# Seven block products for eight in the two feed-forwards of a decoder layer

## The chip, the cores and the metric

The kernel is one program on one core of a Trainium2 chip. A time is what the device takes for one execution, in microseconds (us). TensorE (PE) multiplies matrices into PSUM, which has eight banks of 512 columns; VectorE (DVE) and ScalarE (ACT) do the elementwise work, GpSimd (POOL) a few small operations; SyncE (SP) issues the loads and stores. "PEld" in the profile is TensorE's loading of the stationary operand.

## The reference

One decoder layer for 512 tokens of width 1024: a feed-forward, a mixing layer (attention and a gated delta rule), cross-attention into 256 memory tokens, and a second feed-forward, each between two RMS norms. Everything is float32. The part that matters:

```
def swiglu(x, w_gate, w_up, w_down):
    return (jax.nn.silu(x @ w_gate) * (x @ w_up)) @ w_down        # D_FF = 2816

f = swiglu(rms_norm(h, ffn1_pre_norm[l]), ffn1_w_gate[l], ffn1_w_up[l], ffn1_w_down[l])
h = h + FFN_RESIDUAL_WEIGHT * rms_norm(f, ffn1_post_norm[l])
...
f = swiglu(rms_norm(h, ffn2_pre_norm[l]), ffn2_w_gate[l], ffn2_w_up[l], ffn2_w_down[l])
h = h + FFN_RESIDUAL_WEIGHT * rms_norm(f, ffn2_post_norm[l])
```

## The kernel before

A float32 product is made of three float32r products. `split` (L393) writes `hi` = the operand rounded (ACT) and `lo` = operand - `hi` (DVE); `proj_t` (L486) and `nat_mm` (L504) then multiply hi by hi, hi by lo and lo by hi. So every weight block of 128 x 1024 is loaded by `wload` (L429, three `raw` buffers) and split by `wsplit` (L437) into a pair `wh`, `wl`, of which there are four (`bufs=4`).

A feed-forward is `ffn` (L575). The 2816 hidden columns are 22 chunks of 128. For each chunk, gate and up are two weight blocks, each taken by `proj_t`: 8 slices of the width x 3 matmuls, with the weight slice (128 x 128) stationary and 512 tokens moving, into one bank from `acc` (L370: banks 0 to 5 in turn). In the first feed-forward `lead_in` (L635) does chunks 0 and 1 slice by slice, as x and the weights arrive, and chunk results are later scaled by the row `rb`, since x goes in without its norm. In the second one, chunks 0 and 1 run in two halves of 256 tokens (`HALVES`, L573). `finish` (L580) makes silu(gate) x up of a chunk (tanh on ACT, the rest on DVE) and splits it into `hh` and `hl`.

The down projection is `nat_product` (L509): the hidden chunk is stationary (128 tokens at a time), 512 output columns move. For each of two halves n of the output it goes through 11 weight blocks (two chunks each), for four token tiles t, with four banks accumulating; the last four blocks of n = 1 (`ntail`) are walked one token tile after another. When a bank is complete, `evac` in `residual_epilogue` (L547) squares it for the norm, multiplies it by the gain (`fg`), and with n = 1 done adds the two halves into `h`. Then `next_norm` (L678) and `prenorm` (L467) normalise the tile for the next layer, transpose it on TensorE into banks 6 and 7 (`ptr`), and split it into the four tiles `xt00` to `xt11` (`new_xT`, L458).

Other temporaries are slots of 128 x 512 from a ring of 54 (`u` takes the oldest free one, `fr` gives it back).

No order is written out by hand in the feed-forwards. Every instruction is recorded (the helper's line, L273, is what the profile shows for all of them, so rows are told apart by tile names), and `Issue.settle` (L229) lays them out with costs of its own: a list order for each engine, the instruction on the longest remaining path first, over ten rounds. On the chip each engine then runs its list in order, waiting on semaphores.

## Time and profile before

| | |
|---|---|
| median of 3 runs | 1206.58 us (1205.96 to 1206.93) |
| the profiled execution | 1206.45 us, span 1204.7 us |
| mean granted TensorE clock | 0.999 |
| busy: PE, PEld, DVE, ACT | 1187.5, 989.9, 644.7, 482.0 us |
| matmuls | 6290 |
| first feed-forward | from 6.1 to about 370 us |
| second feed-forward | from about 838 us to the end |

The profile is of one execution. A row of grouped instructions gives the line, the engine, the operation, what it writes and reads, shapes, count, total busy time, mean time of one in ns, and idle time before. Instructions on one engine overlap a little: a busy time runs from an instruction's start to its end, and the next may start earlier. The spacing of starts is read from the order of time.

### The profile page before, as it was taken

The numbers are of one execution on the slowest core, as the hardware profiler recorded it, in microseconds if no ns is written. First come the engines' busy times: TensorE is split into PE (matmuls) and PEld (weight loads), VectorE is DVE, ScalarE is ACT, GpSimd is POOL, SyncE is SP. The second block draws the span as 40 slices with busy tenths as digits, with TensorE's granted clock in tenths as the row PEclk, the third lists the DMA queues.
The fourth block names the chain that finished last, engine by engine and source line by source line (L and its number), as shares of the span: only waits on it lengthen the run. The fifth ranks groups of instructions, "written<-read, shape, count | busy, mean of one in ns | idle before, by whom it ended". The sixth has DMA issues, their size and how long they took to land.

```text
span 1204.7 us, 15978 instructions
## 1 busy us (share of the span) xinstructions
PE 1187.5 (99%) x6290; PEld 989.9 (82%) x6290; DVE 644.7 (54%) x1206; ACT 482.0 (40%) x982; POOL 46.2 (4%) x66
## 2 busy tenths in 40 slices
PE   7999999999999999999999999999999999999997
PEld 6888888888888887887778988888888888888886
DVE  5655454532237977759974955547433443432223
ACT  6323232321225573568863644444323232322211
POOL 0000000000001010101000000002000000000000
PEclk9999999999999999999999999999999999999999
DMA  8333323232433333112242462222323323232321
GB/s 292 113 95 98 105 88 105 97 114 89 121 87 103 126 93 93 56 24 85 81 149 71 139 198 84 73 85 70 106 94 98 101 92 104 97 114 88 105 70 70
DMA packets 48156, 122.61 MB, mean 102 GB/s; under 512 B 9744, under 2 KB 16272, under 8 KB 48080
## 3 DMA queue, kind: packets, MB, share of 16 engines
q1 hardware_dynamic: 47568, 121.45, 31.9%
q8 instruction: 49, 0.80, 0.3%
q0 software_dynamic: 512, 0.13, 0.1%
q14 instruction: 27, 0.22, 0.1%
HBM read 117.11 MB, written 4.33 MB: 101 GB/s over the span
## 4 chain that ended last, share of the span: by engine, by line
PE 89%; DVE 6%; ACT 3%; DMA 1%; POOL 1%; issue 1%; SPq 0%; DVEq 0%; POOLq 0%; ACTq 0%
PE psum L273 89%; DVE p L273 1%; DVE wl L273 1%; POOL smalls L273 1%; DVE h L273 1%; DVE xn L273 1%; DVE pt L273 1%; ACT pt L273 0%; DVE xt L273 0%; DMA mr<-in_mem_dram 0%; ACT wh L273 0%; ACT p L273 0%; DVE smalls L273 0%; ACT u L273 0%; DMA w<-in_f1a_dram 0%
## 5 line engine op out<-in xcount | busy, mean ns | idle before, releaser
L273 PE MATMUL psum<-xt,wh 128*128 128x512 f32 (+1 forms) x2000 | 591.4, 379 | 6.3 <-ACT wh L273 6.3
L273 PEld LDWEIGHTS psum<-xt,wh 128*128 128x128 f32 x2000 | 365.9, 189 | 72.1 <-ACT wh L273 6.6
L273 ACT ACTIVATE wh<-raw 128x1024 fp32r<-128x1024 f32 x197 | 208.9, 1061 | 524.7 <-PE psum L273 274.9
L273 DVE TENSOR_TENSOR wl<-raw,wh 128x1024 fp32r<-128x1024 f32 x197 | 240.9, 1223 | 281.9 <-ACT wh L273 280.7
L273 PE MATMUL psum<-xt,wl 128*128 128x512 f32 (+1 forms) x984 | 371.2, 382 | 0.0
L273 PEld LDWEIGHTS psum<-xt,wl 128*128 128x128 f32 x984 | 185.7, 189 | 33.6 <-DVE wl L273 0.4
L273 PE MATMUL psum<-wl,hh 128*128 128x512 f32 x352 | 137.1, 389 | 0.0
L273 PE MATMUL psum<-wh,hl 128*128 128x512 f32 x352 | 137.0, 389 | 0.0
L273 PE MATMUL psum<-wh,hh 128*128 128x512 f32 x352 | 137.0, 390 | 0.0
L273 PEld LDWEIGHTS psum<-wl,hh 128*128 128x128 f32 x352 | 66.1, 188 | 13.7
L273 PEld LDWEIGHTS psum<-wh,hl 128*128 128x128 f32 x352 | 66.1, 188 | 13.6
L273 PEld LDWEIGHTS psum<-wh,hh 128*128 128x128 f32 x352 | 66.1, 188 | 13.5
L273 POOL TENSOR_TENSOR smalls<-smalls,mhalf 128x1 f32<-128x1 f32 (+1 forms) x38 | 31.5, 829 | 700.8 <-DVE smalls L273 700.5
L273 PE MATMUL psum<-wh,xt 128*128 128x512 f32 x128 | 45.4, 412 | 0.1
L273 DVE SCALAR_TENSOR_TENSOR hv<-s,psum 128x512 f32<-128x512 f32 x22 | 15.1, 688 | 51.6 <-PE psum L273 51.4
L273 DVE TENSOR_TENSOR tu<-psum,rb 128x512 f32<-128x512 f32 x22 | 15.2, 690 | 48.9 <-PE psum L273 48.9
L273 ACT ACTIVATE u<-psum 128x512 f32<-128x512 f32 x32 | 19.0, 594 | 49.3 <-PE psum L273 49.2
L273 DVE TENSOR_TENSOR tg<-psum,rb 128x512 f32<-128x512 f32 x22 | 15.2, 690 | 41.1 <-PE psum L273 41.1
L273 ACT ACTIVATE hh<-hv 128x512 fp32r<-128x512 f32 x44 | 27.4, 623 | 14.2 <-DVE hv L273 14.2
L273 DVE TENSOR_TENSOR hl<-hv,hh 128x512 fp32r<-128x512 f32 x44 | 30.1, 685 | 0.0
L273 DVE TENSOR_TENSOR fg<-psum,gbc 128x512 f32<-128x512 f32 x32 | 21.9, 686 | 13.1 <-ACT u L273 13.1
L273 PEld LDWEIGHTS psum<-wh,xt 128*128 128x128 f32 x128 | 23.4, 189 | 4.3 <-DVE sgz L273 0.4
(234 smaller groups left out, 1356.1 us busy)
## 6 DMA issues: line engine op xcount, KB each, us to landing
raw<-in_f2gu_dram SPq DMA_DIRECT2D x44, 512.0 KB, 3.5
raw<-in_f1gu_dram SPq DMA_DIRECT2D x40, 512.0 KB, 3.6
raw<-in_f1d_dram SPq DMA_DIRECT2D x22, 512.0 KB, 3.5
raw<-in_f2d_dram SPq DMA_DIRECT2D x22, 512.0 KB, 3.5
raw<-in_wmt_dram SPq DMA_DIRECT2D x21, 512.0 KB, 3.5
raw<-in_wmn_dram SPq DMA_DIRECT2D x8, 512.0 KB, 3.5
raw<-in_wout_dram SPq DMA_DIRECT2D x8, 512.0 KB, 3.5
raw<-in_wkvk_dram SPq DMA_DIRECT2D x8, 512.0 KB, 3.5
```

The costliest lines, as they stand in the source:

```text
L273: r = call(*args, **kw)
```

## The change

Two matrices cut into 2 x 2 blocks can be multiplied with seven block products instead of eight, at the price of sums of blocks before and after (Winograd's form of Strassen's scheme: four sums on each side, seven products). The change does so in two places of both feed-forwards.

*Down projection.* `nat_product` is replaced by `down_seven` for all 22 chunks. The first 16 chunks are eight pairs: the left operand's blocks are 256 tokens x one chunk, the right one's one chunk x 512 columns. All eight banks accumulate at once: a (P1 and on), b, c, d, two token tiles each. A first pass over the eight pairs makes four of the products, a second pass, which loads three quarters of the weights again, the other three. The remaining six chunks follow as before, into the same banks, now with all four token tiles and both halves n complete only at the end. The loads of the passes go into the space of `xt00` to `xt11`, which gate and up no longer need (`homes`; pair 0 of the first pass uses the `raw` buffers). Hidden chunks of the pairs stay unsplit until then (`hfs`), and `down_sums` makes the sums of their blocks.

*Gate and up.* Chunks 4 and 5, 8 and 9, 12 and 13, 16 and 17 are made by `seven`, once for gate and once for up: blocks of 128 hidden columns x half the width, and half the width x 256 tokens. Its matmuls have 256 moving columns, 12 to a product. The sums of x are made once per feed-forward, by `seven_k` from the first one's arriving x (which now is scaled by the gain in place and kept) and by `seven_x` from copies of the normalised x that `prenorm` leaves (`keep`, a further ACT copy of each transposed bank). The sums of the weights are made on DVE in the `raw` buffers.

The core of the diff; `...` marks what is left out (helpers that pick halves and quarters of a tile, the loops that free slots, and `seven_x`, which does what `seven_k` does in additions of 512 and splits of 256):

```diff
+NPAIR = 8
+QUADS = (4, 8, 12, 16)
...
-    def prenorm(src, g, dst):
+    def prenorm(src, g, dst, keep=None):
...
+            if keep:
+                A.activation(keep(j), tp, AF.Copy)
             split(dst(j, 0), dst(j, 1), t3)
...
+    def seven_k(xk_):
+        parts = [[[u(F32R, "sx") for _ in range(2)] for _ in range(2)] for _ in range(4)]
+        for k in range(4):
+            a11, a21 = (xk_[k][:, hs] for hs in HALVES)
+            a12, a22 = (xk_[4 + k][:, hs] for hs in HALVES)
...
+            V.tensor_tensor(s1, a21, a22, ALU.add)
+            V.tensor_tensor(s2, s1, a11, ALU.subtract)
+            V.tensor_tensor(s3, a11, a21, ALU.subtract)
+            V.tensor_tensor(s4, a12, s2, ALU.subtract)
+            for i, x_ in enumerate((s1, s2, s3, s4)):
+                split(*(quarter(parts[i][q][k // 2], k % 2) for q in range(2)), x_)
...
+    def seven(wb, wa, xT, sx):
+        right, left = wload(wa), wload(wb)
+        b12, b22, b11, b21 = right[:, 0:512], right[:, 512:1024], left[:, 0:512], left[:, 512:1024]
...
+        w0, w1, w2, w3 = pair(), pair(), pair(), pair()
+        t2 = u(s="t2")
+        split(*half(w0, 0), b11)
+        V.tensor_tensor(b11, b12, b11, ALU.subtract)
+        V.tensor_tensor(t2, b22, b11, ALU.subtract)
+        split(*half(w0, 1), t2)
+        V.tensor_tensor(b12, b22, b12, ALU.subtract)
+        split(*w1, left)
+        V.tensor_tensor(t2, b21, t2, ALU.subtract)
+        split(*w2, right)
+        split(*half(w3, 0), t2)
...
+        a_, b_, c_ = acc(), acc(), acc()
...
+        product(a_, half(w0, 0), plain(0, top), True)
+        A.activation(p1, pa, AF.Copy)
+        product(b_, half(w0, 1), summed(1), True)
+        V.tensor_tensor(u2, pb, p1, ALU.add)
+        product(c_, half(w1, 0), summed(0), True)
+        A.activation(p5, pc, AF.Copy)
+        product(a_, half(w1, 1), plain(1, top), False)
+        A.activation(quarter(out_[0], 0), pa, AF.Copy)
+        product(b_, half(w2, 0), summed(2), False)
+        V.tensor_tensor(u3, pb, p1, ALU.add)
+        V.tensor_tensor(quarter(out_[1], 1), u3, p5, ALU.add)
+        product(c_, half(w2, 1), summed(3), False)
+        V.tensor_tensor(quarter(out_[1], 0), pc, u2, ALU.add)
+        product(b_, half(w3, 0), plain(1, low), False)
+        V.tensor_tensor(quarter(out_[0], 1), pb, p1, ALU.add)
...
+    def down_seven(hfs, hT, wd, evac):
+        a = [acc(), acc()]
+        b = [bank(7), acc()]
+        c = [acc(), acc()]
+        d = [bank(6), acc()]
...
+        for p in range(NPAIR):
+            left, right = ((load if p else wload)(wd[n, p]) for n in range(2))
...
+            V.tensor_tensor(b12, b12, b11, ALU.subtract)
+            V.tensor_tensor(b22, b22, b12, ALU.subtract)
+            V.tensor_tensor(b21, b21, b22, ALU.subtract)
+            w11, w4 = halves(wsplit(left))
+            w1, w2 = halves(wsplit(right))
+            x1, x2, s12, _ = hfs[p]
+            own, sums = parts(x1[:, 256:512], x2[:, 0:256]), parts(s12)
...
+            product(a, own, 0, w11, p == 0)
...
+            product(b, sums, 256, w2, p == 0)
...
+            product(c, sums, 0, w1, p == 0)
...
+            product(d, own, 256, w4, p == 0)
...
+        for p in range(NPAIR):
+            left, right = load(wd[0, p][:, 512:1024]), load(wd[1, p])
...
+            V.tensor_tensor(b12, b22, b12, ALU.subtract)
+            w21, _ = halves(wsplit(left, n=512))
+            w3, w22 = halves(wsplit(right))
+            _, x2, _, s34 = hfs[p]
+            own, sums = parts(x2[:, 256:512]), parts(s34)
+            product(a, own, 0, w21)
+            product(b, sums, 0, w3)
+            product(c, sums, 256, w22)
...
+        w = {(i, n): wblock(wd[n, NPAIR + i]) for i in (rest - 2, rest - 1) for n in (0, 1)}
+        for t in range(NT):
+            for n in (1, 0):
+                for i in (rest - 2, rest - 1):
+                    others(t, n, i, w[i, n], i == rest - 1)
...
+                if more is None:
+                    evac(n, t, ps)
+                else:
+                    V.tensor_tensor(more, ps, more, ALU.add)
+                    evac(n, t, more)
...
+            if len(hfs) < 2 * NPAIR:
+                hfs.append(hv)
+                return
...
+        while i < NFF:
+            if i in QUADS:
+                pg, pu = (seven(wgu[2 * i + j], wgu[2 * i + 2 + j], xT, sx) for j in range(2))
+                for j in range(2):
+                    finish(pg[j], pu[j], True)
+                i += 2
+                if i > max(QUADS):
...
+                    down_sums()
+                continue
...
-        nat_product(
-            list(range(NFF)),
...
+        down_seven(hfs[::2], hT, wd, residual_epilogue(gpost, 0.5, nxt, final))
...
-            fr(xr, wr)
+            fr(wr)
+            V.tensor_scalar(xr, xr, gcol[:, k : k + 1], None, ALU.mult)
```

## Rows read from the trace of the kernel before

**Rows 1.** The page, part 1: busy us (share of the span) xinstructions.

```profile
PE 1187.5 (99%) x6290; PEld 989.9 (82%) x6290; DVE 644.7 (54%) x1206; ACT 482.0 (40%) x982; POOL 46.2 (4%) x66
```

**Rows 2.** The chain that ended last: start us, length us, what.

```profile
6.11 349.65 PE psum L273 x1536
...
844.90 353.52 PE psum L273 x1621
```

**Rows 3.** Windows: stretch, its length, busy us (x) of each engine, PEclk, DMA share, GB/s.

```profile
25.00:250.00 225.00, 225.00 (x999) 186.49 (x998) 121.53 (x156) 71.22 (x89) 0.56 (x2) 1.00 0.32 102
...
850.00:1068.00 218.00, 218.00 (x1007) 182.45 (x1006) 89.30 (x105) 64.50 (x83) 0.00 (x0) 1.00 0.32 102
1078.00:1198.00 120.00, 120.00 (x531) 99.39 (x530) 33.67 (x37) 25.38 (x34) 2.02 (x3) 1.00 0.26 85
```

**Rows 4.** What PE waited for: us in total, times, longest us.

```profile
PE psum L273 <- ACT wh L273: 6.3, 2, 6.1
```

**Rows 5.** PE in order of time, 512 columns: start us, us, instruction xcount.

```profile
990.16 0.61 PE L273 MATMUL psum<-xt,wh 128*128 128x512 f32 x2
...
990.84 0.61 PE L273 MATMUL psum<-xt,wh 128*128 128x512 f32 x2
```

**Rows 6.** PE in order of time, 256 columns (six matmuls between these starts).

```profile
842.55 0.40 PE L273 MATMUL psum<-xt,wh 128*128 128x256 f32 x2
...
843.27 0.40 PE L273 MATMUL psum<-xt,wh 128*128 128x256 f32 x2
```

**Rows 7.** DVE in order of time, first feed-forward: start us, us, instruction [idle before].

```profile
31.37 1.23 DVE L273 TENSOR_TENSOR wl<-raw,wh 128x1024 fp32r<-128x1024 f32 x1 [2.49 <-ACT wh L273]
32.51 0.68 DVE L273 TENSOR_TENSOR tg<-psum,rb 128x512 f32<-128x512 f32 x1
33.12 0.68 DVE L273 TENSOR_TENSOR tu<-psum,rb 128x512 f32<-128x512 f32 x1
...
107.35 0.69 DVE L273 TENSOR_TENSOR tu<-psum,rb 128x512 f32<-128x512 f32 x1 [2.69 <-PE psum L273]
108.08 0.69 DVE L273 SCALAR_TENSOR_TENSOR hv<-s,tu 128x512 f32<-128x512 f32 x1
```

**Rows 8.** DVE groups by shape: xcount | busy us, mean ns | idle before, releaser.

```profile
L273 DVE TENSOR_TENSOR wl<-raw,wh 128x1024 fp32r<-128x1024 f32 x197 | 240.9, 1223 | 281.9 <-ACT wh L273 280.7 <-DMA raw<-in_wmt_dram 0.8
...
L273 DVE TENSOR_TENSOR v<-psum,v 128x256 fp32r<-128x256 f32 x8 | 3.3, 416 | 0.1
...
L273 DVE TENSOR_SCALAR gbc<-gbc 128x512 f32<-128x512 f32 x4 | 1.7, 427 | 12.5 <-DMA gbc<-in_gains_dram 12.5
```

**Rows 9.** ACT groups by shape.

```profile
L273 ACT ACTIVATE wh<-raw 128x1024 fp32r<-128x1024 f32 x197 | 208.9, 1061 | 524.7 <-PE psum L273 274.9 <-issue 233.5 <-DMA raw<-in_wkvk_dram 5.5
L273 ACT ACTIVATE hh<-hv 128x512 fp32r<-128x512 f32 x44 | 27.4, 623 | 14.2 <-DVE hv L273 14.2
...
L273 ACT ACTIVATE xt<-psum 128x512 fp32r<-128x512 f32 x24 | 13.5, 589 | 9.8 <-PE psum L273 8.8 <-DVE smalls L273 0.9
...
L273 ACT ACTIVATE v<-psum 128x256 fp32r<-128x256 f32 x8 | 3.1, 383 | 3.4 <-PE psum L273 2.0 <-DVE v L273 1.2
```

**Rows 10.** Windows, stretches where DVE is loaded most.

```profile
5.50:28.00 22.50, 21.89 (x87) 17.95 (x88) 15.28 (x27) 17.90 (x34) 2.21 (x4) 1.00 0.91 339
28.00:50.00 22.00, 22.00 (x102) 18.36 (x102) 15.83 (x22) 8.71 (x12) 0.00 (x0) 1.00 0.36 120
...
356.00:374.00 18.00, 17.42 (x89) 13.67 (x87) 15.82 (x29) 11.71 (x28) 5.24 (x7) 1.00 0.11 38
820.00:838.00 18.00, 17.84 (x98) 14.90 (x96) 16.13 (x28) 11.42 (x26) 4.69 (x6) 1.00 0.16 51
```

**Rows 11.** DMA issues: KB each, median us from issue to landing.

```profile
raw<-in_f1d_dram SPq DMA_DIRECT2D x22, 512.0 KB, 3.5
```

**Rows 12.** One weight split in order of time, ACT then DVE.

```profile
101.73 1.06 ACT L273 ACTIVATE wh<-raw 128x1024 fp32r<-128x1024 f32 x1 [3.17 <-PE psum L273]
...
102.83 1.22 DVE L273 TENSOR_TENSOR wl<-raw,wh 128x1024 fp32r<-128x1024 f32 x1 [0.23 <-ACT wh L273]
```

## What bounds the kernel, what the change should do, and the prediction

> **What bounds the kernel now.** I read the page's first part first: TensorE (PE) is busy for 99% of the span, VectorE (DVE) for 54%, ScalarE (ACT) for 40% [rows 1]. A busy PE need not be a full one, so next comes the chain that ended last: its two longest pieces are unbroken PE work and are the two feed-forwards, 349.65 us from 6.11 and 353.52 us from 844.90 [rows 2]. Cut by stage, the granted clock is 1.00 (the 2.4 GHz level) throughout, and PE is busy for 225.00 of 225, 218.00 of 218 and 120.00 of 120 us [rows 3]. All PE idling on ACT's weight splits is 6.3 us, 6.1 of it one wait, the start of the kernel [rows 4]. So in both feed-forwards the end is set by the number of matmuls times their spacing, and DVE and ACT have room there: 121.53 and 71.22 us in the 225, 33.67 and 25.38 in the 120 [rows 3].
>
> Spacing is read from starts, since busy times overlap. With 512 columns three matmuls take 990.84 - 990.16 = 0.68 us, 0.2267 each [rows 5]. With 256 columns, each still with a weight load of its own, six take 843.27 - 842.55 = 0.72 us, 0.120 each [rows 6]: 6% more per column.
>
> **TensorE's part.** Down, per feed-forward: 22 chunks x 4 token tiles x 2 halves x 3 matmuls = 528 before. After, 8 pairs x 7 products x 6 = 336, and 6 plain chunks x 24 = 144: 480. Saved 48 x 0.2267 = 10.9 us. Gate and up: `seven` does one weight matrix of two chunks, 7 products x 12 matmuls of 256 columns = 84 x 0.120 = 10.08 us, in place of 2 x 24 x 0.2267 = 10.88. Saved 0.80, eight times per feed-forward: 6.4. Sum for two feed-forwards: 2 x 17.3 = **34.6 us**. Only about a third of what seven-for-eight promises in gate and up survives the shorter matmul.
>
> The Trainium skill ("TensorE: Matmul & The Clock Gate", Back-to-back issue gap) gives an isolated spacing of N/2.4 + 2.5 ns when warm, so 109 ns at 256 and 216 at 512 columns. By that, an estimate, the sum would be 16 x 1.2 + 96 x 0.216 = 39.8 us; the rows show 120 and 227, and they decide.
>
> **What the other engines get.** Start to start, DVE needs 1.14 us for 1024 elements and 0.60 for 512 [rows 7]; the line through both gives 0.33 for 256, whose busy time is 416 ns from PSUM [rows 8]. That is the term with no row of its own (no 256-wide SBUF operation of two tensors is there); bounds are 0.27, the slope alone, and the busy 0.42. I take 0.33, since the two rows it is drawn through are the same operation. ACT's busy times are 1.06, 0.62 and 0.38 for 1024, 512 and 256 [rows 9].
>
> The Trainium skill ("VectorE: DVE Perf Modes", the section on the TRN2 errata) has (58 + elements)/0.96 ns for an operation from SBUF, 327 ns at 256; with it the sums below would not move.
>
> `seven`: 4 subtractions and 3 `lo` parts of 512 (7 x 0.605), 2 `lo` of 1024 (2.28), 5 evacuations of 256 (1.65): 8.2 us of DVE in 10.08 of PE. With the two chunks' `finish` (4.8 in the first feed-forward, which scales by `rb`, 2.4 in the second) a group of four chunks, two of them plain, needs 16.4 + 4.8 + 4.6 + 4.8 = 30.6 of DVE in 42 us of PE. It is hidden, if it may slide within the group. Buffers allow that: all four `wh`/`wl` pairs go into one `seven`, but the next one's w0 comes free 2.9 us into the first and is wanted at 10.08, its w3 at 10.08 and wanted at 18.7; no more than 6.5 us of weight work stands between. Tightest is PSUM bank b: u3 must be read within the 12 matmuls of the next product, 1.44 us; that read is 0.42, but may stand behind a 1.14 us operation. I put 0.15 us on each of 16: 2.4 us (0 to 8).
>
> Sums of x: 16 additions and 16 `lo` of 256 (10.6 us DVE), and in the first feed-forward 8 scalings of 512 at 0.43 [rows 8]: 14 us more before the first `seven`, where DVE is busy for 15.28 of 22.5 and 15.83 of 22 us [rows 10]. The room, 13.4 us, is just used up; three of the four sums and some finishing can wait. 1 us (0 to 4). In the second feed-forward four chunks of plain work cover it; its eight ACT copies (`keep`, 0.59 each) fall where ACT has 11.42 of 18 us [rows 10]: 0.7 us (0 to 3).
>
> `down_seven`, first pass, per pair: 3 subtractions (1.8), 2 `lo` of 1024 (2.28), splits of 512 and 2 x 256 (0.60 + 0.67): **5.37 us DVE against 24 x 0.2267 = 5.44 of PE**. Second pass: 3.3 against 4.08, and `down_sums` (32 x 0.33 = 10.6) lies beside four plain chunks with 43.5 us: hidden. The first pass has no room. A dependent operation starts 0.73 after the one ahead instead of 0.60 [rows 7], and where DVE is hardest pressed today it is busy for 88% and 90% of its time (15.82 and 16.13 of 18) [rows 10]. At 90% a pair takes 5.97 us, 0.53 too long, for 14 pairs 7.4 us; at 98.7% nothing. I take the middle, 3.7.
>
> Entry into the pass: loads for pair 1 go into xT's space, freed by the 12th matmul before the end of gate and up's last 24, so 2.72 + 5.44 = 8.16 us before PE wants them. A 512 KB load lands in 3.5 us [rows 11], the second 1.5 later (512 KB at the 339 GB/s of [rows 10]); three subtractions 1.8, `hi` 1.1 [rows 12], `lo` 1.14, some 0.4 of signals: 9.4. Late by 1.3, twice: 2.6 us (0 to 6).
>
> Boundary to the mixing layer: at the end all four weight buffers serve to the last token tile, so the next projection's first block is split 1.36 us before the end and is ready (1.1 + 1.14 + signals) about 1.2 us late. DVE gains 4 `fg` and 6 additions in this tail (6 us), but token tile 0 is done 5.4 us earlier than today. 1.2 us (0 to 4). After the last matmul nothing changes: 1204.7 - 1198.4 = 6.3 us stays.
>
> **Sum.** Stalls 2.4 + 1 + 0.7 + 3.7 + 2.6 + 1.2 = 11.6 us, bounds 0 to 32. Profiled execution 1206.45 us (span 1204.7), 0.13 under the median 1206.58, so no correction: 1206.45 - 34.6 + 11.6 = **1183.5**. My forecast's own range is 1177 to 1192.
>
> **Rivals.**
> A, everything hides: stalls under 5 us, the planner's order fills each gap as it does before (PE loses 0.6 us in the first boundary [rows 10]). Against it: 98.7% of DVE in the first pass. 1172 to 1177, say 1174.
> B, DVE becomes the bound in the first pass at 90% and in the sevens too, with the bounds of most terms taken: stalls 20 to 32. 1192 to 1204, say 1197.
> C, slower: DVE and ACT hand each split over in order. ACT's `hi` starts at 101.73, DVE's `lo` at 102.83 [rows 12], so 1.10 us a block if DVE has nothing between; 0.66 for 512, 0.42 for 256. A first-pass pair has 2 x 1.10 + 0.66 + 2 x 0.42 = 3.7 us of handovers. If half were open, a pair would take 7.2 us, +1.8 x 16 = 28; one of the second pass (2.8 us of them) 4.7, +0.6 x 16 = 10; `seven` (4.2 us of them) 10.3, +0.2 x 16 = 3.5; with 8 for entry and boundaries 49.5: 1221. It decides from about 40% open on. For it: today DVE does wait on ACT's `hi` before most `lo` (281.9 us idle, [rows 8]). Against: that is in stages with room, and under pressure DVE keeps 88 to 90%.
> D, slower too: loads that run one behind the other. The first pass wants 1 MB per 5.44 us, 193 GB/s. Were each load to wait for the one ahead, 7.0 us a pair, +1.6 x 16, second pass 7.0 against 4.08, +2.9 x 16: 1206.45 - 34.6 + 72 = 1244. Against: 339 GB/s in one stretch [rows 10], eight homes.
> That the change does not do what it says I hold for excluded: the counts follow from its loops, and 256-column spacing is a row.
>
> **How the numbers follow.** Forecast 0.50, A 0.18, B 0.20, C 0.08, D 0.04. The range takes in the forecast, most of A and most of B: **1174 to 1200**. About 0.2%, 2.4 us, is what a measurement of this kernel can tell from no change. Faster: forecast, A and B, 0.88; same 0.03, from between B and C; slower 0.09.
>
> **What would show it.** Right: some 480 more matmul records (2 x (672 - 384 - 48)), 256-column ones 0.12 apart in the sevens; the first pass's pairs 5.4 to 6.0 us apart, the second's at 4.1; a PE gap of about 1 us at the first pass's second pair, released by DVE; DVE near 880 us busy (2 x 116 more), clock still 1.00. Wrong: the 256-column spacing above 0.13, which kills gate and up's part; pairs at 7 us (C or D, told apart by what ended the wait, `hi` or a load); PE waits inside each `seven`; a granted clock below 1.00 in the feed-forwards.

## The result, and the profile after

| | before | changed |
|---|---|---|
| median | 1206.76 us (1205.96 to 1207.41) | 1189.12 us (1186.91 to 1191.58) |
| ratio | | 0.9855, 95% interval 0.9834 to 0.9875 |
| profiled execution | 1206.45 us, clock 0.999 | 1191.58 us, clock 0.991 |

The change gains 17.6 us, where 34.6 - 11.6 = 23.0 was predicted. The profiled execution is the longest of the four, with a gain of 14.9; the accounts below are made against it. In the changed kernel the helper's line is L276 (L277 where an experiment adds a line).

The page of the changed kernel, part 1 (busy us, share, instructions) and the row of the granted clock from part 2 (40 slices), answering to [rows 1]:

```profile
PE 1161.4 (98%) x6770; PEld 995.0 (84%) x6770; DVE 880.7 (74%) x1694; ACT 586.5 (49%) x1206; POOL 46.7 (4%) x66
...
PEclk9999999989998999999999999999999999998999
```

The counts are as predicted: 480 matmuls more, VectorE at 880.7 us (some 880 was forecast). New are three 8s in the row of the clock. The windows say where they lie and what stands around them (columns as in [rows 3]):

```profile
24.00:60.00 36.00, 34.73 (x180) 29.56 (x179) 34.91 (x72) 17.59 (x36) 1.54 (x2) 1.00 0.29 88
60.00:230.00 170.00, 170.00 (x1045) 153.64 (x1045) 140.20 (x226) 68.13 (x98) 0.00 (x0) 1.00 0.35 106
```

```profile
236.50:250.70 14.20, 11.16 (x50) 8.90 (x48) 6.88 (x13) 3.99 (x10) 0.00 (x0) 0.97 0.77 280
250.70:257.60 6.90, 6.84 (x18) 5.43 (x19) 6.90 (x13) 4.30 (x7) 0.00 (x0) 0.57 0.76 237
257.60:300.00 42.40, 42.34 (x186) 34.43 (x185) 40.20 (x61) 29.21 (x49) 0.00 (x0) 1.00 0.56 167
1063.00:1076.90 13.90, 10.66 (x48) 8.48 (x46) 6.39 (x11) 3.23 (x6) 0.00 (x0) 0.96 0.77 292
1076.90:1083.80 6.90, 6.82 (x18) 5.38 (x19) 6.76 (x9) 4.72 (x9) 0.00 (x0) 0.58 0.54 147
...
366.80:373.70 6.90, 5.88 (x31) 5.59 (x30) 5.61 (x10) 3.25 (x7) 2.40 (x2) 0.57 0.35 96
```

From 60 to 230 us, where the sevens are, TensorE is busy for 170.00 of 170 (in the second feed-forward for 231.00 of 231, from 832 us on). It stops for about 3 us at each entry into a first down pass (11.16 of 14.20, 10.66 of 13.90). Right after each stop, and after the boundary to the mixing layer, the granted clock is one half, the 1.2 GHz level, for 6.8 us. At the first entry the record has it from 249.80 to 256.62 us; the windows shown begin about 1 us later than these stretches and so read 0.57 and 0.58. In the first of them two matmuls of 512 columns stand 0.42 us apart, for 0.227 before the stop. Its first 1.0 us is still the stop; in the 5.9 us behind that 14 matmuls start, each some 0.2 us later than at full clock: 2.8 us, nearly as much again as the stop. At the second entry it is 2.8 us as well (13 matmuls), at the boundary some 2.5 (5.8 us of work, 256 columns 0.213 us apart for 0.120; an estimate).

To see by stage what was gained, the starts of TensorE's first and last matmul of each stage are enough. The table is worked out from them, in us, for the profiled execution of every kernel of this study. "Gate, up 1" runs from the first matmul to the first down product, "passes" are the two passes of `down_seven` over the eight pairs (8 x (5.44 + 4.08) = 76.2 if nothing stops), "down" is the whole down projection, "edge" from its last product to the mixing layer's first matmul, "layers" from there to the last matmul of cross-attention, where the edits change nothing but a few small operations (the copies of `keep`; e3, e5).

| kernel | gate, up 1 | passes 1 | down 1 | edge | layers | gate, up 2 | passes 2 | down 2 | execution |
|---|---|---|---|---|---|---|---|---|---|
| before | 242.5 | – | 121.9 | 0.2 | 463.4 | 244.5 | – | 119.5 | 1206.45 |
| changed | 238.0 | 82.7 | 118.0 | 3.3 | 465.6 | 237.3 | 82.2 | 114.8 | 1191.58 |
| e4 gate and up alone | 237.0 | – | 121.9 | 0.2 | 470.2 | 236.9 | – | 119.5 | 1200.61 |
| e5 down alone | 242.8 | 79.3 | 113.9 | 3.3 | 464.9 | 243.1 | 80.8 | 113.4 | 1196.15 |
| e1 fourth raw buffer | 237.1 | 85.5 | 121.5 | 4.5 | 462.3 | 237.4 | 83.5 | 116.1 | 1194.01 |
| e2 other list order | 237.5 | 80.2 | 117.2 | 3.7 | 466.1 | 238.2 | 77.6 | 110.2 | 1187.40 |
| e9 = e1 + e2 | 238.3 | 77.7 | 113.6 | 2.9 | 465.1 | 237.4 | 78.3 | 110.9 | 1182.52 |
| e10 = e9 + VectorE work | 240.3 | 77.7 | 114.9 | 3.5 | 463.3 | 237.2 | 76.0 | 108.6 | 1182.12 |
| e3 constants early | 241.1 | 81.8 | 116.8 | 3.0 | 467.9 | 239.4 | 82.2 | 115.4 | 1197.90 |
| e11 = e9 + five groups | 237.2 | 77.6 | 113.0 | 3.8 | 468.1 | 235.5 | 78.1 | 110.7 | 1182.70 |
| e12 = e11, later landing | 236.8 | 77.3 | 113.1 | 3.8 | 468.1 | 235.8 | 76.2 | 108.9 | 1181.17 |
| e13 = e12 + GpSimd | 236.3 | 76.8 | 113.6 | 3.6 | 467.2 | 235.4 | 77.2 | 109.8 | 1180.93 |
| e14 = e12 - additions | 236.0 | 77.4 | 112.6 | 2.7 | 464.8 | 235.3 | 76.6 | 109.3 | 1175.93 |
| e15 = e12, six groups | 235.1 | 78.6 | 114.5 | 2.7 | 461.9 | 233.7 | 78.3 | 111.0 | 1172.67 |

Of the change's gains, gate and up keep 4.5 + 7.2 of 12.8; the down projections only 3.9 + 4.6 of 21.8; edge and layers lose 3.1 + 2.2.

How the stop at the entry comes about is read from VectorE's list. VectorE and TensorE of the changed kernel in order of time (start, length, instruction, [idle before, what ended it]):

```profile
244.07 0.69 DVE L276 TENSOR_TENSOR tu<-psum,rb 128x512 f32<-128x512 f32 x1 [2.53 <-PE psum L276]
248.21 0.69 DVE L276 TENSOR_TENSOR xw<-xw 128x512 f32<-128x512 f32 x1 [3.44 <-DMA xw<-in_f1d_dram]
248.81 0.68 DVE L276 SCALAR_TENSOR_TENSOR hv<-s,tu 128x512 f32<-128x512 f32 x1
249.41 0.69 DVE L276 TENSOR_TENSOR xw<-xw 128x512 f32<-128x512 f32 x1
250.02 0.69 DVE L276 TENSOR_TENSOR sl<-s,sh 128x512 fp32r<-128x512 f32 x1
```

```profile
247.27 0.39 PE L276 MATMUL psum<-wl,sh 128*128 128x512 f32 x1
250.76 2.50 PE L276 MATMUL psum<-wh,sl 128*128 128x512 f32 x5 [3.10 <-DVE sl L276]
253.06 0.63 PE L276 MATMUL psum<-wh,sh 128*128 128x512 f32 x1
253.48 0.63 PE L276 MATMUL psum<-wl,sh 128*128 128x512 f32 x1
```

This is the first entry. TensorE is at pair 0 and wants its `sl`, whose operands are ready. But in VectorE's list two subtractions of pair 1's weights (`xw`) stand ahead of it, and the first waits 3.44 us for its load. The chain of waits gives that load 6.22 us; the DMA view of 236 to 262 us gives the median of ten:

```profile
241.96 6.22 DMA xw<-in_f1d_dram
```

```profile
GB/s 0 85 183 199 88 416 240 0 0 69 227 403 422 410 309 391 410 429 359 391 403 441 422 422 410 391 107 50 69 88 284 340 107 195 309 214 19 0 0 0
...
xw<-in_f1d_dram SPq DMA_DIRECT2D x10, 512.0 KB, 6.8
```

xT's space becomes free within 3 us, so eight loads of 512 KB are issued within 5.0 us (the row's ten include two later ones), and while they run the queues move some 400 GB/s. The ten land after 6.8 us in the median instead of the 3.5 of [rows 11]. The planner, which counts about 3.5 us for every such load (2.1 of landing behind 1.45 of cost), placed the subtraction accordingly. The Trainium skill ("HBM Reference", Specifications (TRN2)) gives about 425 GB/s to a core that streams alone, bounded by its 16 DMA engines; the trace agrees (359 to 441 in all but two slices of the burst). By that figure eight loads would take 8 x 0.524 MB / 425 GB/s = 9.9 us, an estimate; the burst in the row lasts 16 slices of 0.65, 10.4 us.

At the second entry pair 0 is complete, and TensorE waits for `wh` of pair 1:

```profile
1072.06 0.69 DVE L276 TENSOR_TENSOR xw<-xw 128x512 f32<-128x512 f32 x1 [3.12 <-DMA xw<-in_f2d_dram]
1073.34 1.29 DVE L276 TENSOR_TENSOR xw<-xw 128x512 f32<-128x512 f32 x2 [0.58 <-DMA xw<-in_f2d_dram]
...
1075.15 0.69 DVE L276 TENSOR_TENSOR xw<-xw 128x512 f32<-128x512 f32 x1
...
1075.87 1.06 ACT L276 ACTIVATE wh<-xw 128x1024 fp32r<-128x1024 f32 x1 [5.74 <-DVE xw L276]
...
1076.98 1.22 PE L276 MATMUL psum<-wh,sh 128*128 128x512 f32 x2 [3.32 <-ACT wh L276]
```

By the semaphores of the trace, the first subtraction is pair 1's, and the second waits for a load of pair 2; it and an `hl` stand between pair 1's three. Three subtractions in a row (0.60 each) and `hi` (1.06) would have had `wh` ready 1.4 us after TensorE wanted it (1072.06 + 2.86, against 1068.06, where pair 0 began, + its 5.44). So of the 3.32 us some 1.4 are pair 1's own lateness and 1.9 the order of the list, an estimate. At the first entry pair 1 by itself would have been 1.8 us late in the same count (248.21 + 2.86, against 243.87 + 5.44).

### The profile page after: what moved, and what is told of

It reads as the page before. It is cut to its first block, busy times and chain, and to the rows that moved or that the text cites. A ratio compares the mean times of both kernels' runs of the same rounds, so it can differ in the third digit from the quotient of the medians.

```text
span 1189.5 us, 17848 instructions
## 1 busy us (share of the span) xinstructions
PE 1161.4 (98%) x6770; PEld 995.0 (84%) x6770; DVE 880.7 (74%) x1694; ACT 586.5 (49%) x1206; POOL 46.7 (4%) x66
## 4 chain that ended last, share of the span: by engine, by line
PE 83%; DVE 7%; DMA 4%; ACT 3%; issue 1%; SPq 0%; POOL 0%; DVEq 0%; POOLq 0%; ACTq 0%
PE psum L276 83%; DVE wl L276 1%; DVE p L276 1%; DMA x<-in_xt_dram 1%; ACT u L276 1%; ACT wh L276 1%; DVE pt L276 1%; DMA xw<-in_f2d_dram 1%; DVE h L276 1%; DMA xw<-in_f1d_dram 1%; DMA h<-in_x_dram 1%; SPq L276 0%; DMA mr<-in_mem_dram 0%; ACT k L276 0%; DVE xn L276 0%
## 5 line engine op out<-in xcount | busy, mean ns | idle before, releaser
L276 PE MATMUL psum<-xt,wh 128*128 128x512 f32 (+1 forms) x1872 | 506.3, 358 | 8.6 <-ACT wh L276 6.9
L276 PEld LDWEIGHTS psum<-xt,wh 128*128 128x128 f32 x1872 | 331.2, 191 | 55.4 <-ACT wh L276 7.2
L276 PE MATMUL psum<-xt,wl 128*128 128x512 f32 (+1 forms) x920 | 325.7, 359 | 0.0
L276 ACT ACTIVATE wh<-raw 128x1024 fp32r<-128x1024 f32 (+1 forms) x185 | 189.0, 1022 | 241.5 <-PE psum L276 192.2
L276 DVE TENSOR_TENSOR wl<-raw,wh 128x1024 fp32r<-128x1024 f32 (+1 forms) x185 | 217.5, 1175 | 121.2 <-ACT wh L276 119.4
L276 PEld LDWEIGHTS psum<-xt,wl 128*128 128x128 f32 x920 | 175.2, 191 | 23.0
L276 PE MATMUL psum<-sx,wh 128*128 128x256 f32 x512 | 93.5, 283 | 0.0
L276 PE MATMUL psum<-wh,sl 128*128 128x512 f32 x224 | 87.7, 399 | 3.1 <-DVE sl L276 3.1
L276 PE MATMUL psum<-wl,sh 128*128 128x512 f32 x224 | 87.5, 394 | 0.0
L276 PE MATMUL psum<-wh,sh 128*128 128x512 f32 x224 | 84.1, 405 | 3.4 <-ACT wh L276 3.3
L276 PEld LDWEIGHTS psum<-sx,wh 128*128 128x128 f32 x512 | 79.9, 192 | 0.0
L276 ACT ACTIVATE wh<-xw 128x1024 fp32r<-128x1024 f32 (+1 forms) x60 | 55.8, 938 | 38.0 <-PE psum L276 15.9
L276 DVE TENSOR_TENSOR wl<-xw,wh 128x1024 fp32r<-128x1024 f32 (+1 forms) x60 | 64.4, 1077 | 12.2 <-ACT wh L276 12.1
L276 PE MATMUL psum<-sx,wl 128*128 128x256 f32 x256 | 72.4, 283 | 0.0
L276 POOL TENSOR_TENSOR smalls<-smalls,mhalf 128x1 f32<-128x1 f32 (+1 forms) x38 | 31.9, 840 | 685.3 <-DVE smalls L276 684.9
L276 PEld LDWEIGHTS psum<-wh,sh 128*128 128x128 f32 x224 | 43.6, 196 | 13.9 <-ACT wh L276 4.7
L276 PEld LDWEIGHTS psum<-wh,sl 128*128 128x128 f32 x224 | 43.3, 194 | 12.6 <-DVE sl L276 3.5
L276 PEld LDWEIGHTS psum<-wl,sh 128*128 128x128 f32 x224 | 42.8, 191 | 9.1
L276 PEld LDWEIGHTS psum<-sx,wl 128*128 128x128 f32 x256 | 49.2, 192 | 0.0
L276 ACT ACTIVATE wh<-t 128x512 fp32r<-128x512 f32 x32 | 20.2, 630 | 52.5 <-DVE t L276 23.9
L276 PE MATMUL psum<-wh,xt 128*128 128x512 f32 x128 | 45.3, 411 | 0.1
L276 DVE TENSOR_TENSOR xw<-xw 128x512 f32<-128x512 f32 x58 | 39.6, 685 | 7.3 <-DMA xw<-in_f2d_dram 3.7
```

The source lines that it names most:

```text
L276: r = call(*args, **kw)
```

## The experiments

Every edit makes the planner lay out the whole program anew. The column "layers" shows what that alone does: code that was hardly edited takes from 461.9 to 470.2 us, part of it at the low clock (e11 and e12 have 10.2 us of that there). So an edit's effect is read from its own stage, and a difference of a few us between two medians proves nothing about the edit.

**Which half of the change.** e4 keeps gate and up, e5 the down projection (`...` where `down_sums` is replaced by plain splits):

```diff
e4 -        down_seven(hfs[::2], hT, wd, residual_epilogue(gpost, 0.5, nxt, final))
e4 +        nat_product(list(range(NFF)), ..., wd, 2, residual_epilogue(gpost, 0.5, nxt, final), 4, ...)
e5 -QUADS = (4, 8, 12, 16)
e5 +QUADS = ()
```

> Only gate and up use seven products; the down projection is the one of before (the hidden chunks of the first sixteen are split after the last group instead of being summed). Theory (gate and up give their full gain, 2 x 6.4 us, less 1 to 2 us at the first group): 1206.6 - 12.8 + 1.5 = 1195. Rival (DVE cannot keep up in the groups, 30.6 of 42 us, or PSUM bank b stops PE): 1200 or more.

> Only the down projections use seven products; gate and up are those of before, without the sums of x and without the copies of the normalised x. Theory (down's gain of 2 x 10.9 us loses 2 x 6 us at the entries, stop and slow clock together, and 5 us at the boundary): 1206.6 - 21.8 + 17 = 1202. Rival (the losses come from gate and up's sums crowding DVE, down itself runs clean): 1190 or less.

e4: 1201.28 us (ratio 0.9956, 0.9941 to 0.9971), 6 above the 1195 that were expected. Gate and up by themselves gain 5.5 and 7.6, 13.1 in sum for the 12.8 that the spacings of [rows 5, 6] gave: that term is settled. The execution shows 5.8 of it, since "layers" is 6.8 longer. e5: 1196.53 us (0.9918, 0.9903 to 0.9933), 5.5 below what was expected of it. Down gains 8.0 and 6.0 of 10.9 each, and the edge costs 3.1 as in the whole change: the edge belongs to the down projection.

**What stops TensorE at the entry.** e1 gives pair 1 of the first pass `raw` buffers, whose loads needn't wait for xT's space. e2 leaves all code as it is, and has the planner count 4.7 us of landing for a load into that space instead of 2.1 (6.2 us in all instead of 3.5), by which only the order of the lists changes.

```diff
e1 -NSLOT = 54            +NSLOT = 52
e1 -tag="raw", bufs=3     +tag="raw", bufs=4
e1 -((load if p else wload)(wd[n, p]) for n in range(2))
e1 +((load if p > 1 else wload)(wd[n, p]) for n in range(2))
e2 +        "DMAW": (4700, 4700, 4700),     # beside "DMA": (2100, 2100, 2000)
```

> Pair 1 of the first down pass is loaded into the raw buffers (four of them instead of three, 52 slots instead of 54) and so no longer waits for the space of xT. Theory (late load and a blocked list): in the changed kernel DVE stands before pair 1's subtraction, whose load lands 6.2 us after its issue, and pair 0's lo part is behind it in DVE's list; PE stops for 3.3 and 3.5 us and comes back at the 1.2 GHz level for 6.8 us each time. With early loads both stops fall under 1 us, both slow stretches go, and the time falls from 1189 by 8 to 13 us, to about 1178. Rival (DVE is the bound of the first pass, 5.37 of 5.44 us a pair): the stop moves to a later pair, the two passes stay at 82 us, and the time falls by under 4 us.

> The planner counts a load into the space of xT (tiles xw) with 4.7 us of landing time in place of 2.1; nothing else changes, so it alters only list orders. Pair 0's lo part now stands ahead of pair 1's first subtraction in DVE's list, which it did not before. Theory (blocked list): the stop within pair 0 goes, and what is left is pair 1's own lateness, a stop of 1.5 to 3 us before pair 1 with a shorter slow-clock stretch; the two down stages together lose 9 us instead of 13, the total falls to about 1185. Rival (only the late loads matter, whoever stands behind them): the stops keep their 3.3 us and move from pair 0 to pair 1; same time as the changed kernel, 1189. The mixing layer's order is laid out anew as well and may shift the total by -1 to +7 us, so the down stages are read by themselves.

e1: 1193.40 us (0.9890, 0.9875 to 0.9904), worse than the change, a miss. TensorE's stop in pair 0 of the first entry is 6.44 us there. Its VectorE:

```profile
243.87 0.69 DVE L276 TENSOR_TENSOR tu<-psum,rb 128x512 f32<-128x512 f32 x1 [1.35 <-PE psum L276]
250.47 0.69 DVE L276 TENSOR_TENSOR xw<-xw 128x512 f32<-128x512 f32 x1 [5.91 <-DMA xw<-in_f1d_dram]
...
253.42 0.75 DVE L276 TENSOR_TENSOR sl<-hv,sh 128x256 fp32r<-128x256 f32 x2
```

Pair 1 is early now, but the planner has put pair 2's subtraction in the same place, ahead of the pair 0 work that TensorE wants. Pair 2 isn't wanted until two pairs are done; the reader of its load stands too early. e2: 1185.36 us (0.9821, 0.9807 to 0.9836), as expected. There the order in pair 0 is turned round:

```profile
245.19 0.69 DVE L277 TENSOR_TENSOR sl<-s,sh 128x512 fp32r<-128x512 f32 x1
...
246.79 0.69 DVE L277 TENSOR_TENSOR xw<-xw 128x512 f32<-128x512 f32 x1
248.08 1.30 DVE L277 TENSOR_TENSOR xw<-xw 128x512 f32<-128x512 f32 x2 [0.60 <-DMA xw<-in_f1d_dram]
```

The longest wait for a load is 0.60 us, and the passes take 80.2 and 77.6 us for 82.7 and 82.2. The stop for `sl` is gone. What is left at the first entry is the stop that was expected before pair 1, 2.28 us for `wh`, with 3.4 us at the low clock; at the second it is 0.77 us. Same code, same buffers, same work: the order took 7.1 us off the passes, and the late load by itself makes only a part of the change's stops. Not all of this is VectorE's list: in the second feed-forward the new order also issues the first loads 5.5 us ahead of the first down product instead of 2.8, and what that gave was not measured by itself. Of the 2.28 us a part is order again, since a subtraction of pair 2 (248.08, behind the wait of 0.60) and an `sl` still stand between pair 1's three.

**Both together, and VectorE's room.** e9 takes both edits. e10 adds one subtraction of 512 per pair of the first pass to it, whose result nobody reads; VectorE then has 5.37 + 0.60 = 5.97 us a pair for TensorE's 5.44.

```diff
e10 +            scr = u(s="scr")
e10 +            V.tensor_tensor(scr, b11, b22, ALU.subtract)
e10 +            fr(scr)
```

> Both: pair 1 loaded early into the raw buffers (four instead of three, 52 slots), and the planner told of 4.7 us for the loads into the space of xT. Theory (late loads times a blocked list, nothing else wrong with the first pass): no stop over 1 us at either entry, no slow-clock stretch there, the two passes take 77 us instead of 82 each, and the total comes to 1174 to 1181. Rival (DVE with 5.37 of 5.44 us a pair is the bound as soon as the entry is mended): the passes stay above 80 us with many short stops, 1186 or more.

> As e9_raw4_order, and one more DVE subtraction of 128 x 512 (0.60 us, its result unused) for each pair of the first pass, 16 in all. If the first pass is DVE-bound (5.37 + 0.60 against 5.44), each pair after the first takes 0.53 us more: 14 x 0.53 = 7.4 us over e9_raw4_order. If DVE works far enough ahead in the stages around it (the rival), under 2 us more.

e9: 1184.28 us (0.9813, 0.9797 to 0.9828), above the 1174 to 1181 that were expected, and one stop over 1 us stays, 2.03 us for `sl` at the second entry. The passes do fall to 77.7 and 78.3, 8.9 us together, and its profiled execution is 9.1 shorter than that of the change. Two of its other executions lose it again at mean clocks of 0.991 and 0.992 (profiled: 0.996), and the median is that of e2 within the intervals. The stops at the two entries, in us: 3.10 and 3.32 in the change, 6.44 and 3.09 with the early load alone (e1), 2.28 and 0.77 with the other order alone (e2), 0.72 and 2.03 with both. So the early load does harm without the order, helps with it at the first entry, and does not help at the second.

e10: 1186.05 us (0.9835, 0.9808 to 0.9861), not 7.4 over e9 but 1.8, within the intervals; its passes are no longer, 77.7 and 76.0. The window from 262 to 310 us of the changed kernel, then of e9, then of e10:

```profile
262.00:310.00 48.00, 47.94 (x211) 39.53 (x211) 48.00 (x74) 31.31 (x51) 0.00 (x0) 1.00 0.61 181
```

```profile
262.00:310.00 48.00, 48.00 (x212) 39.32 (x211) 47.12 (x73) 29.72 (x48) 0.00 (x0) 1.00 0.53 166
```

```profile
262.00:310.00 48.00, 48.00 (x213) 39.77 (x212) 48.00 (x75) 31.93 (x51) 0.00 (x0) 1.00 0.51 170
```

In the changed kernel and in e10 VectorE is busy without a gap, and TensorE stops for no more than 0.06 us of the 48. So VectorE does not bound the first pass: over both passes it needs 8 x (5.97 + 3.3) = 74 us even with the addition, under 76.2, and work for later pairs can be taken ahead.

**The edge to the mixing layer.** In the changed kernel TensorE waits there for the normed row; the windows are of about the last 16 us of the down projection and the 8 after it, first before, then changed:

```profile
356.00:372.00 16.00, 15.65 (x76) 12.15 (x74) 14.27 (x25) 11.44 (x27) 4.23 (x6) 1.00 0.04 14
372.00:380.00 8.00, 7.78 (x62) 7.38 (x62) 7.55 (x14) 3.44 (x8) 2.06 (x3) 1.00 0.54 172
```

```profile
347.00:363.00 16.00, 14.62 (x72) 11.63 (x70) 15.31 (x29) 9.98 (x26) 3.16 (x5) 1.00 0.00 1
363.00:371.00 8.00, 5.11 (x23) 4.39 (x24) 7.16 (x11) 6.06 (x13) 2.54 (x2) 0.68 0.42 133
```

```profile
364.87 0.55 PE L276 MATMUL psum<-ident,xn 128*128 128x128 f32 x3 [2.58 <-DVE xn L276]
```

VectorE is full in the last 16 us (15.31, for 14.27 before), TensorE idle for 4.3 us of the 24 (0.6 before). Three explanations were tried. e3: constants of the mixing layer, for whose loads VectorE and ACT wait in their lists up to 343 and 344 us (1.3 and 5.2 us), are loaded ahead of the first feed-forward. e13: the gain's multiplication of six results per feed-forward goes to GpSimd. e14: the six additions of kept halves are left out, so that a part of the down projection's sum is missing.

```diff
e3  -    (cr, gr, cw, gob, coef: loads and scalings)   behind the first ffn(...)
e3  +    (the same lines)                              ahead of it
e13 -            V.tensor_tensor(fg[n, t], ps, g[n], ALU.mult)
e13 +            (V if ps.tensor.name.startswith("psum") else G).tensor_tensor(fg[n, t], ps, g[n], ALU.mult)
e14 -                    V.tensor_tensor(more, ps, more, ALU.add)
e14 -                    evac(n, t, more)
e14 +                    evac(n, t, ps)
```

> The small constants of the mixing layer (coef, gob, cw, cr, gr) are loaded and scaled ahead of the first feed-forward instead of at its end; nothing else changes. Theory: at the boundary ACT stands 5.2 us before coef's load and DVE 1.3 us before gob's while token tile 0's result is waiting, which delays the norm chain by 2 us; without them PE's stop of 2.6 us before the mixing layer shrinks to about 1 us, and the slow-clock stretch after it may go too: 2 to 5 us less, 1184 to 1187. Rival (the 6 us of additional DVE work in the tail sets the stop): under 1 us less.

> As the run with 6.4 us, and the multiplication by the gain of the six results of each feed-forward that lie in SBUF is done by GpSimd instead of VectorE (about 6 x 0.7 us less on VectorE at the end of a feed-forward). Theory (VectorE's added work at the end of the second pass holds back xn, on which TensorE waits at the boundary to the mixing layer): last down product to first product of the mixing layer shrinks by 1.5 to 3 us, and the end of the kernel by 1 us; 3 to 4 us under the run with 6.4 us. Rival (GpSimd takes longer for one than VectorE, so that the results leave later): the boundary is as long or longer, 0 to 4 us over it.

> As the run with 6.4 us, but the six additions that join the kept half of a block's result to the half of the second pass are left out in each feed-forward: that part of the down projection's sum isn't computed, and the time is to be read as that of VectorE with 6 x 0.6 us less at the end of each feed-forward. Theory (these additions hold back xn at the boundary): the time from the last down product to the first of the mixing layer, and the stops just before and after it, shrink by 2 to 4 us together, the time by 2 to 5. Rival (the boundary is set by the order of the results and by the chain from the last result to xn, whatever stands beside): under 1 us less.

e3 stands on the changed kernel: 1196.42 us (0.9912, 0.9895 to 0.9929). The edge stays at 3.0, so the constants aren't the cause; the time is 7 us longer than the change's, gate and up taking 3.1 and 2.1 more and the layers 2.3. e13: 1182.69 us (0.9800, 0.9779 to 0.9820), where 3 to 4 less than e12 was expected; edge 3.6 for e12's 3.8, within the intervals no change. A multiplication takes GpSimd 1.30 us, VectorE 0.68. e14: 1178.06 us (0.9771, 0.9754 to 0.9787), 2.5 under e12 with overlapping intervals. The two windows answering to those above, of e12 and of e14:

```profile
341.00:357.00 16.00, 14.74 (x72) 11.65 (x71) 15.39 (x28) 9.78 (x27) 3.47 (x6) 1.00 0.01 1
357.00:365.00 8.00, 4.89 (x23) 3.98 (x24) 7.93 (x14) 6.30 (x12) 1.33 (x3) 0.79 0.32 98
```

```profile
340.60:356.60 16.00, 15.51 (x79) 12.56 (x78) 14.06 (x26) 11.53 (x30) 2.75 (x5) 1.00 0.00 1
356.60:364.60 8.00, 5.15 (x37) 4.31 (x35) 7.12 (x11) 4.41 (x10) 2.92 (x2) 1.00 0.44 131
```

Without the additions VectorE is less full (21.18 us of 24 for 23.32), TensorE less idle (3.3 us for 4.4), the edge 1.1 shorter, and the clock stays at 1.00. So VectorE's added work seems to hold up part of the edge, as far as one kernel with an order of its own shows it. What sets the remaining 2.7 us isn't settled; the chain from the last result through square, root, normed row and transposition was not taken apart.

**More groups.** e11 is e9 with five groups of seven products instead of four, e12 counts 6.4 us of landing instead of 4.7, e15 is e12 with six groups.

```diff
e11 -QUADS = (4, 8, 12, 16)                e11 +QUADS = (5, 8, 11, 14, 17)
e12 -        "DMAW": (4700, 4700, 4700),   e12 +        "DMAW": (6400, 6400, 6400),
e15 -QUADS = (5, 8, 11, 14, 17)            e15 +QUADS = (5, 7, 10, 12, 15, 17)
```

> As e9_raw4_order, with five groups of two chunks in seven products instead of four (chunks 5, 8, 11, 14 and 17 on), one plain chunk between them in place of two, and the first group one chunk later. Theory: one more group saves 1.6 us per feed-forward, and the later start takes the stop of 1.3 us before the first group away: 4 us under e9_raw4_order. A group of three chunks then asks 25.9 of 31.0 us of DVE in the first feed-forward; if DVE is the bound there (rival), it is no faster or slower than e9_raw4_order.

> The previous version (four raw buffers, seven-product chunks 5, 8, 11, 14, 17) with one number more changed: the planner counts 6.4 us for a load into the space of xT instead of 4.7. Only the order of the engines' lists changes. Theory (the subtraction of a pair stands in VectorE's list too early, since its load lands later than the list assumes): the stop of 2.0 us at the entry of the second feed-forward's first pass goes below 0.7 us, nothing else gets longer, 1178 to 1179.5 us. Rival (the loads then start or land later in the same measure, or the order of another stage becomes worse): a stop of 2 us or more stays, or the layers between grow by 2 us, 1180 to 1184.

> As the run with five seven-product chunk pairs and 6.4 us, with six of them in each feed-forward, beginning at chunks 5, 7, 10, 12, 15 and 17, so that two stand one behind the other three times. Theory (a group costs TensorE 20.16 us for 21.76, whatever stands beside, and VectorE's and ScalarE's work slides within the plain chunk between): 2 x 1.6 = 3.2 us less in the two gate and up stages, 1177.3 us. Rival (VectorE needs 21.2 us for a group in the first feed-forward, so that two in a row make it the bound, or the weight pairs come late): stops inside the sevens appear, gate and up of the first feed-forward gains under 0.5 us, 1179 to 1182.

e11: 1180.94 us (0.9785, 0.9767 to 0.9804), 3.3 under e9 for 4 expected; gate and up are 1.1 and 1.9 shorter (1.6 each by the count). The wait for `tg` ahead of the first group did not go with the later start: 2.2 us, for 1.3 in the change. At the second entry a stop of 1.8 us was left. First e11, then e12, VectorE there:

```profile
1068.63 0.69 DVE L277 TENSOR_TENSOR xw<-xw 128x512 f32<-128x512 f32 x1 [1.33 <-DMA xw<-in_f2d_dram]
1069.89 1.29 DVE L277 TENSOR_TENSOR xw<-xw 128x512 f32<-128x512 f32 x2 [0.57 <-DMA xw<-in_f2d_dram]
...
1072.04 0.68 DVE L277 TENSOR_TENSOR sl<-s,sh 128x512 fp32r<-128x512 f32 x1
```

```profile
1068.38 0.76 DVE L277 TENSOR_TENSOR sl<-hv,sh 128x256 fp32r<-128x256 f32 x2 [0.76 <-ACT sh L277]
1069.06 1.29 DVE L277 TENSOR_TENSOR xw<-xw 128x512 f32<-128x512 f32 x2
1070.26 0.69 DVE L277 TENSOR_TENSOR sl<-s,sh 128x512 fp32r<-128x512 f32 x1
```

In e12 these two waits for loads are gone (one of 0.19 us is left behind them), and the passes of the second feed-forward take 76.2 us, which is the count of matmuls and nothing else: there the mechanism of the entry is closed. Those of the first take 77.3, with a stop of 0.93 us for `sl`. The median, 1180.55 us (0.9784, 0.9765 to 0.9803), is that of e11 all the same, above the 1178 to 1179.5 that were expected: the 1.9 us of the second passes do not show in executions that scatter by 5.7, which the last section comes back to.

e15: 1172.70 us (1172.31 to 1174.80; 0.9724, 0.9711 to 0.9738), the shortest of the study, 33.7 us under before and 16.4 under the change. The sixth group gave 1.7 and 2.1 us in gate and up for 1.6 each, and TensorE has no stop among the groups:

```profile
58.00:240.00 182.00, 182.00 (x1278) 171.38 (x1277) 167.56 (x280) 83.89 (x130) 0.00 (x0) 1.00 0.33 106
```

VectorE is at 167.56 of 182 us there. The other 4 to 5 us by which e15 beats the 1177.3 expected lie in "layers", 6.2 shorter in this layout, and are no merit of the edit; its passes are even longer again, 78.6 and 78.3.

## Why the prediction held, and where its steps failed

The time, 1189.1 us, lies in the range, 5.6 above the forecast, and the sign and the main mechanism (number of matmuls times spacing) are right. But the stalls were 34.6 - 14.9 = 19.7 us in the profiled execution where the sum had 11.6, in other places than it said. That the time came so near is partly luck: bank b, copies and drift were to cost 6.8 us together and cost none, while entry and edge cost 18.6 where 3.8 was forecast, each of them above its own bounds (0 to 6 and 0 to 4).

| step | predicted | profile | read from |
|---|---|---|---|
| bank b in the sevens | 2.4 | 0 | 170.00 of 170, 231.00 of 231 us busy |
| sums of x, first group | 1 | 1.9 | gate, up 1: 4.5 of 6.4 (1.3 a wait for `tg`) |
| copies, second start | 0.7 | -0.8 | gate, up 2: 7.2 of 6.4 |
| drift in the first pass | 3.7 | 0 | 47.94 of 48 us busy; e12's passes 2, 76.2 |
| entry into the first pass | 2.6 | 13.3 | down: 3.9 + 4.6 of 21.8 |
| edge to the mixing layer | 1.2 | 5.3 | edge 3.1, layers 2.2 |

- **TensorE's part** was right to a few tenths: the counts, and the spacing in the new kernel. Between the first and the second of these rows lie three matmuls, 0.36 us:

```profile
60.08 0.40 PE L276 MATMUL psum<-sx,wh 128*128 128x256 f32 x2
...
60.44 0.40 PE L276 MATMUL psum<-sx,wh 128*128 128x256 f32 x2
```

The 109 ns of the Trainium skill ("TensorE: Matmul & The Clock Gate", Back-to-back issue gap), and with it 39.8 us, did not appear: with a weight load for each matmul it is 120, here as before. e4 measured the gate and up part directly, 13.1 for 12.8. Only an aside is wrong: 0.80 of the 1.36 us that seven for eight promises for a weight matrix of two chunks is three fifths, not a third.

- **VectorE's prices** were right: an operation of 256 columns from SBUF, which had no row, starts 0.33 to 0.34 us after the one ahead:

```profile
30.41 0.42 DVE L276 TENSOR_TENSOR sxf<-x,x 128x256 f32<-128x256 f32 x1
30.74 0.42 DVE L276 TENSOR_TENSOR sxf<-x 128x256 f32<-128x256 f32 x1
31.08 0.42 DVE L276 TENSOR_TENSOR sxf<-sxf,x 128x256 f32<-128x256 f32 x1
```

- **Drift** was the wrong step of principle. 88 to 90% busy in the old kernel was taken as VectorE's ceiling; those were stretches with less work, not with a limit. It runs at 48.00 of 48 us (the changed kernel, e10) with TensorE unhindered. That disposes of rival B in its place (the stalls come close to its 20 us, but not for its reason), and of C: the handovers were covered.
- **Entry** was under-sized five-fold, the clock included. The chain of pair 1 (load, subtraction, split) was priced by a load that runs almost alone, 3.5 us, the next 1.5 later; issued as a burst, the loads take 6 to 7 us. By itself that makes pair 1 late by some 1.8 and 1.4 us (above), not far from the 1.3 that was forecast for each. But it was priced as if only pair 1 would be late, and only by its own chain. On an engine that works its list in order, a reader of a late load also delays everything behind it: at the first entry pair 0's `sl`, needed at once, at the second pair 1's own next subtractions. e2 shows the first: with another order the stop for `sl` goes, and 2.28 us before pair 1 are left. Rival D (loads one behind the other throughout) did not come; its idea, that the loads hinder each other, did, once per feed-forward.
- **The clock** had no price. A clock below 1.00 was named as what would make the prediction wrong, and it came: three stretches of 6.8 us after three stops, 2.8 + 2.8 + 2.5 = 8.1 us of the 19.7. The stops of the entries themselves are 3.10 us (for `sl`) and 3.32 us (for `wh`); with 2 x 2.8 of the clock that is 12.0 of the 13.3. Another 0.7 is a stop at 351 us, near the end of the down projection, for the normed row, and belongs to the edge.
- **Edge.** The sum had one late weight split, 1.2 us. It came, 1.02 us:

```profile
369.02 1.22 PE L276 MATMUL psum<-xt,wh 128*128 128x256 f32 x4 [1.02 <-ACT wh L276]
```

The larger wait is for the normed row, 2.58 us, behind a VectorE that is full with the added epilogue (e14). Neither this nor the 2.5 us of the clock behind it was in the sum; in "layers", 2.2 longer, the new order gave some 1.3 back. What else makes the edge is open.

## What to carry to other kernels

When an edit frees space for many loads at one time, price the first reader by the whole burst, and look at what stands behind that reader in its engine's list: the reader waits for its load, and innocent work behind it waits too. Here one corrected landing cost in the planner took 7.1 us off the passes, and another buffer without it added 4.1. An engine's busy share in an old stretch isn't its ceiling. Where a layout is searched anew after each edit, compare stages, not medians; stages that were hardly edited moved by 8 us here.

## What the runs showed of the hardware that was not expected

After stops of TensorE the granted clock was at the 1.2 GHz level for 3.4, 6.8 or (e1, after 6.44 us of stop) 10.2 us. The length of the stop alone does not decide it: stops of 2.23 us (e5), 2.03 (e9) and 1.57 (e15) at an entry were followed by 1.00, those of 2.28 us (e2, at an entry) and 1.39 us (e12, in the mixing layer, at 563 us) by 3.4 us at the low level. What decides it no run here shows. The same program differs from execution to execution by it. The four executions of e12 have spans of 1175.7, 1178.1, 1179.4 and 1181.4 us at mean clocks of 0.999, 0.996, 0.995 and 0.994: 5.7 us between the ends, and 0.005 x 1180 = 5.9. It is not the whole of it: two executions of the changed kernel span 1187.1 us, at 0.991 and at 0.995. The kernels with the change scatter by 2 to 7 us here; the one before, whose longest stop behind its start is 1.5 us, by 2 at most. Rows of such a stretch are no prices of instructions.
